# Sample attention scores and value products in plain float32 matmuls, without splits

## The chip, the cores and the metric

The kernel runs on one core of a Trainium2 chip. The metric is the device time of one execution in microseconds; the median of three runs stands for a kernel. Engines are named as in the profile: PE (matrix multiply), PEld (its weight loads), DVE (vector), ACT (scalar), POOL (GpSimd), SP (the queue that issues the transfers).

## The reference

One inference step of a one-layer hybrid encoder: 1024 prompt frames of one new stream and 16 new frames for each of 8 running streams, model width 1024. The change touches the attention of the running streams (the sample): 8 heads of 64, 512 cached frames per stream plus the 16 new ones, no softmax but a stick-breaking weight:

```python
z = jnp.einsum('bqhd,bkhd->bhqk', q, k) * (HEAD_DIM ** -0.5)
log_fail = jnp.where(mask, jax.nn.log_sigmoid(-z), 0.0)
log_between = lax.cumsum(log_fail, axis=3, reverse=True) - log_fail
a = jnp.where(mask, jnp.exp(jax.nn.log_sigmoid(z) + log_between), 0.0)
return jnp.einsum('bhqk,bkhd->bqhd', a, v)
```

Everything is float32. Around it lie an input projection, the same attention over the prompt, a pooling branch, gates, an output projection, and a convolutional feed-forward part.

## The kernel before

All tokens (128 sample rows and 1024 prompt rows) go through the input projection, the pooling branch, the prompt attention, then the sample attention woven with branch A of the later tokens, the output projection and the feed-forward part, one after the other on one core.

**Precision by splits.** PE multiplies operands of type `F32R` in one pass. To keep float32 precision the kernel splits a tensor into a high part, a copy into an `F32R` tile, and a low part, the difference (`split`, L85), and replaces a product by three matmuls: high × high, high × low, low × high (`mm3`, L118; L119 to L121 in the profile). An operand that is not `F32R`, such as the data of a transpose against the identity, is multiplied in plain float32.

**The sample attention** works on one stream (a batch b, 0 to 7) at a time, with keys in pairs of heads (p, 0 to 3):

- `s_kload` and `s_vload` issue the loads of cached keys (1 MB) and values (4 × 256 KB) on SP.
- `s_kt` (L781) transposes a pair's 512 keys on PE into a PSUM bank; `s_kth` (L794, ACT) copies it as the high part `kth`, `s_ktl` (L799, DVE) subtracts for the low part `ktl`. Only then the bank is free. `s_new` (L788, DVE) appends the 16 new keys to both.
- `s_qb` (L775, POOL) lays a batch's queries, high and low, into a block-diagonal tile `qb`.
- `s_qk` forms the scores `zs` with `mm3`: columns 256 to 527 first (n = 1, 272 columns), then 0 to 255 (n = 0), four pairs each, 12 matmuls a half. The chain `chain_steps` (L600 to L612) follows: three ACT functions, a sum, a scan and a sum on DVE, an exponential on ACT.
- `s_tr` (L822) transposes the weights on PE; `s_a3` copies their high part (L833, ACT) and subtracts the low part (L831, DVE).
- `s_vh` (L761, DVE) casts a value tile to its high part, `s_vl` (L765, mostly POOL) makes the low part, in tiles borrowed from `mh12`, `ml12` and the prompt's buffers.
- `s_av` multiplies for each quarter j of the keys and each pair: one matmul of both weight parts (64 columns of weights) with the high values (L847), one of the high weights (32 columns) with the low values (L851). `s_ob` and `s_os` bring the four parts out, `s_sum` adds them.

Between these stand `br_half`, the halves of branch A (six split matmuls of 384 columns each), whose results go through `merge_unit`: a gate product (L938, DVE), a sum (L939, POOL), a copy (L940, ACT) and a low part (L941, DVE).

**The order** of this stage is written by hand. Each step is put into a list with a due time (`at_(time, function)`), the list is sorted, and every engine runs its own steps in that order (`tc.manual_schedule`). A period of one batch is 10.6 in these times; they set the order only. Batches 0 to 2 overlap without branch work before batch 2; from batch 2 on a period holds a batch's scores, four key transposes of the next, four branch halves, four value products of the one before, and one transpose of weights.

Of the kernel before, what the change touches and what calls it, by code (L numbers as in the profile page):

```python
# [16 lines left out]
P = 128  # L17
# [22 lines left out]
def trunk_kernel(  # L40
# [421 lines left out]
    s_samp = ExitStack()  # L462
    smp = mk_pool("samp", "left", stack=s_samp)
    qs_h = smp.tile([P, 4, P], F32R, name="qs_h")
    qs_l = smp.tile([P, 4, P], F32R, name="qs_l")
    ks_h = smp.tile([P, 4, P], F32R, name="ks_h")
    ks_l = smp.tile([P, 4, P], F32R, name="ks_l")
# [8 lines left out]
    def qkv_units(p):  # L476
# [66 lines left out]
        def k_tr(ts_):  # L543
# [180 lines left out]
    def s_setup():  # L724
        for i in range(2):
            q_ = p2.tile([P, 2, AW], F32R, tag="ql", bufs=2, name=f"qb{i}")
            for j in range(2):
                pool.memset(f32(q_[:, j, :]), 0.0)
            qb.append(q_)
# [15 lines left out]
    def s_vload(b, j):  # L745
        if b == 6 and j < 2:
            if j == 0:
                vt["x"] = p2.tile([P, 4, AW], F32R, tag="vhl", bufs=2, name="v6")
            vt[b, j] = vt["x"][:, j, :], vt["x"][:, 2 + j, :]
        elif b % 2 == 0:  # L750
            vt[b, j] = mh12[:, 4 + j, :AW], ml12[:, 4 + j, :AW]
        else:
            if j == 0 and b == 1:
                vt["qd"] = [p2.tile([P, 2, AW], F32R, tag=f"qd{k}", bufs=2, name=f"v{'lh'[k]}{b}_{i}")
                            for k in range(2) for i in range(2)]
            vt[b, j] = vt["qd"][j // 2][:, j % 2, :], vt["qd"][2 + j // 2][:, j % 2, :]
        vr[b, j] = p2.tile([P, AW], F32, tag="kvst", bufs=4, name=f"vr{b}_{j}")
        sync.dma_start(vr[b, j], cache_v[0, b, j * P:(j + 1) * P].rearrange("p h d -> p (h d)"))

    def s_vh(b, j):  # L760
        dve.tensor_copy(vt[b, j][1], vr[b, j])  # L761

    def s_vl(b, j):
        lo, hi = vt[b, j]
        (dve if (b == NB - 1 and j > 1) or (b in (4, 6) and j == 0) else pool).tensor_tensor(lo, vr.pop((b, j)), f32(hi), ALU.subtract)  # L765

    def s_qb(b):
        for j, src in enumerate((qs_h, qs_l)):
            for hh in range(2):
                hs = slice(hh * HD, (hh + 1) * HD)  # L770
                q_ = qb[b % 2]
                sv = f32(src[hs].rearrange("p a (t b) -> p a t b", b=NB)[:, :, :, b])
                c0, o = (384, P) if j else (0, 0)
                dst = q_.rearrange("p j c -> p (j c)")[hs, c0:c0 + 640].rearrange("p (a s) -> p a s", s=160)
                pool.tensor_copy(dst[:, :, o + hh * NS:o + (hh + 1) * NS], sv)  # L775
# [8 lines left out]
    def s_new(b, i):  # L784
        for j, (hl, src) in enumerate((("h", ks_h), ("l", ks_l))):
            kt = p2.tile([P, 2, KA], F32R, tag=f"kk{j}", bufs=2, name=f"kt{hl}{b}_{i}")
            bst[b].setdefault(hl, []).append(kt)
            dve.tensor_copy(kt[:, :, PAST:KA],  # L788
# [715 lines left out]
```

## Time and profile before

| | us |
|---|---|
| median of 3 runs | 1776.23 (1775.72 to 1777.47) |
| span of the profiled execution | 1774.7 |
| PE busy in it | 1708.0 |
| sample attention, first cached-key transpose to output projection | 652.10 to 797.76 |

The page gives the profiled execution's span, from its first to its last instruction; a time of its own beside the span is not shown, and the span lies 1.5 us under the median. Times are microseconds from the start of the span. A busy time counts instructions that run; matmuls overlap, so PE may be busy without being at its peak, and the distance of two starts, not the duration, says what a matmul costs in a row of them. "PEclk" is the share of full clock that PE was granted: 1.00 is 2.4 GHz, 0.50 is 1.2 GHz, and a value between is a mean over a stretch with both. What stands behind an arrow is the instruction that ended a wait.

### The profile page before, as it was taken

To read this page: it belongs to the slowest core of one execution; us is meant where nothing else is said; L and a number is where in the kernel's file an instruction comes from. 1 tells how busy PE (TensorE), PEld (TensorE's weight loads), DVE (VectorE), ACT (ScalarE), POOL (GpSimd) and SP (SyncE) were. 2 spreads that over 40 slices of the span, in tenths; PEclk is the share of its full clock that TensorE was granted. 3 is DMA by queue.
4 is the path that set the end of the run, shared out by engine and by line. 5 is a ranking of instruction groups with operands and counts; after the bars stand their busy time and mean duration, and the time that the engine had idled before them with its cause. 6 is when DMAs were issued, how large, how long until landed. Compare 5 with 4: busy or idle time off the path is not lost.

```text
span 1774.7 us, 24393 instructions
## 1 busy us (share of the span) xinstructions
PE 1708.0 (96%) x9785; PEld 1565.1 (88%) x9785; DVE 936.5 (53%) x1311; ACT 753.4 (42%) x1472; POOL 487.9 (27%) x506
## 2 busy tenths in 40 slices
PE   8999999999999997779999999999999999999997
PEld 7999998888888886778889998989989898998995
DVE  5350117778776778894253535345353444535356
ACT  5231127777776775543234332423223242332423
POOL 5111233222222125552412222322213131222222
PEclk9999999999999998989999999999999999999999
DMA  6111131111113125548301110211111111110112
GB/s 184 49 49 63 63 102 54 51 47 39 50 53 119 61 88 201 161 148 267 101 13 36 37 48 24 60 36 48 39 36 48 48 37 47 36 51 25 60 36 110
DMA packets 132942, 125.39 MB, mean 71 GB/s; under 512 B 8625, under 2 KB 113021, under 8 KB 132829
## 3 DMA queue, kind: packets, MB, share of 16 engines
q1 hardware_dynamic: 132829, 123.83, 22.4%
q8 instruction: 77, 1.26, 0.3%
q14 instruction: 36, 0.29, 0.1%
HBM read 101.63 MB, written 21.65 MB: 69 GB/s over the span
## 4 chain that ended last, share of the span: by engine, by line
PE 75%; DVE 15%; ACT 4%; DMA 2%; issue 2%; POOL 1%; SPq 0%; POOLq 0%; DVEq 0%; ACTq 0%
PE up L121 10%; PE up L119 10%; PE up L120 10%; PE dn L119 4%; PE dn L120 4%; PE dn L121 4%; DVE S L607 2%; PE gb L120 2%; PE gb L121 2%; PE gb L119 2%; PE kv L119 2%; PE kv L121 1%; PE kv L120 1%; PE o L119 1%; PE o L120 1%
## 5 line engine op out<-in xcount | busy, mean ns | idle before, releaser
L119 PE MATMUL up<-mh,wup_h 128*128 128x384 f32 x1056 | 353.4, 335 | 0.0
L121 PE MATMUL up<-mh,wup_l 128*128 128x384 f32 x1056 | 353.0, 334 | 0.0
L120 PE MATMUL up<-ml,wup_h 128*128 128x384 f32 x1056 | 352.8, 334 | 0.0
L1371 DVE SCALAR_TENSOR_TENSOR C<-E,convp,C 128x128 f32<-128x128 f32 x88 | 80.4, 913 | 287.1 <-ACT C L1368 278.5
L1428 DVE TENSOR_TENSOR x<-dn,x 128x512 f32<-128x512 f32 x198 | 132.8, 687 | 149.8 <-PE dn L121 149.7
L119 PEld LDWEIGHTS up<-mh,wup_h 128*128 128x128 f32 x1056 | 198.4, 188 | 0.5
L120 PEld LDWEIGHTS up<-ml,wup_h 128*128 128x128 f32 x1056 | 198.3, 188 | 0.3
L121 PEld LDWEIGHTS up<-mh,wup_l 128*128 128x128 f32 x1056 | 198.3, 188 | 0.0
L96 POOL TENSOR_TENSOR wup_l<-wup_r,wup_h 128x1024 fp32r<-128x1024 f32 x44 | 104.9, 2393 | 283.9 <-ACT wup_h L95 244.5
L119 PE MATMUL dn<-wd_h,gh 128*128 128x512 f32 x396 | 158.4, 401 | 2.0 <-DVE x L1428 2.0
L120 PE MATMUL dn<-wd_l,gh 128*128 128x512 f32 x396 | 156.5, 395 | 1.4 <-POOL wd_l L96 1.4
L121 PE MATMUL dn<-wd_h,gl 128*128 128x512 f32 x396 | 156.3, 395 | 0.0
L95 ACT CAST wup_h<-wup_r 128x1024 fp32r<-128x1024 f32 x44 | 45.5, 1050 | 212.8 <-PE dn L121 143.5
L1367 ACT COPY E<-up 128x384 f32<-128x384 f32 (+2 forms) x176 | 65.6, 398 | 151.0 <-PE up L121 151.0
L1372 DVE SCALAR_TENSOR_TENSOR C<-E,convp,C 128x1024 f32<-128x1024 f32 x88 | 112.0, 1273 | 0.0
L119 PEld LDWEIGHTS dn<-wd_h,gh 128*128 128x128 f32 x396 | 74.2, 188 | 25.9 <-DVE x L1428 9.2
L120 PEld LDWEIGHTS dn<-wd_l,gh 128*128 128x128 f32 x396 | 74.4, 188 | 18.5 <-POOL wd_l L96 1.9
L121 PEld LDWEIGHTS dn<-wd_h,gl 128*128 128x128 f32 x396 | 74.4, 188 | 17.9
L1368 ACT ACTIVATE C<-up,convp 128x384 f32<-128x384 f32 x132 | 90.0, 682 | 0.0
L605 DVE SCALAR_TENSOR_TENSOR e<-z,e 128x384 f32<-128x384 f32 (+3 forms) x96 | 53.2, 554 | 62.1 <-ACT e L602 61.4
L119 PE MATMUL kv<-wkv_h,hTh 128*128 128x256 f32 x288 | 85.0, 295 | 0.9 <-DVE ql L506 0.9
L96 POOL TENSOR_TENSOR wd_l<-wd_r,wd_h 128x1024 fp32r<-128x1024 f32 x22 | 52.9, 2403 | 105.0 <-ACT wd_h L95 105.0
(324 smaller groups left out, 4099.7 us busy)
## 6 DMA issues: line engine op xcount, KB each, us to landing
wup_r<-in_w_up_dram SPq DMA_DIRECT2D x44, 512.0 KB
wd_r<-in_w_down_dram SPq DMA_DIRECT2D x22, 512.0 KB
vr<-in_cache_v_dram SPq DMA_DIRECT2D x32, 256.0 KB
kr<-in_cache_k_dram SPq DMA_DIRECT2D x7, 1024.0 KB
sp_tb<-tb SPq DMA_DIRECT2D x8, 576.0 KB
out_dram<-kvst SPq DMA_DIRECT2D x72, 64.0 KB
sp_ga<-ga SPq DMA_DIRECT2D x24, 192.0 KB
tbr<-sp_tb SPq DMA_DIRECT2D x24, 192.0 KB
```

The source lines that it names most:

```text
L95: act.copy(hi, raw)
L96: (pool if how[1] == "p" else dve).tensor_tensor(lo, raw, f32(hi), ALU.subtract)
L119: pe.matmul(ps, lhsT=lh, rhs=rh, start=start, stop=False)
L120: pe.matmul(ps, lhsT=lh, rhs=rl, start=False, stop=False)
L121: pe.matmul(ps, lhsT=ll, rhs=rh, start=False, stop=stop)
L605: dve.scalar_tensor_tensor(ev, z, 0.0, ev, ALU.max, ALU.add)
L607: dve.tensor_tensor_scan(Sv[:, ::-1], ev[:, ::-1], ev[:, ::-1], init, ALU.add, ALU.bypass)
L1367: act.copy(d_, s2_)
L1368: act.activation(C[:, cs], ps, AF.Identity, scale=convp[:, 2, u:u + 1], bias=convp[:, 3, u:u + 1])
L1371: dve.scalar_tensor_tensor(C[:, 0:P], E[:, 16 - 8 * sh:EZ - 8 * sh], wv, C[:, 0:P], ALU.mult, ALU.add)
L1372: dve.scalar_tensor_tensor(C[:, P:T], E[:, EP - sh:EL - sh], wv, C[:, P:T], ALU.mult, ALU.add)
L1428: ins = dve.tensor_tensor(x1[t][:, hs], ps, x1[t][:, hs], ALU.add)
```

## The change

Queries, keys, values and weights of the sample stay plain float32, in one tile each. `mm3` in `s_qk` becomes one plain matmul for each pair, the two value matmuls become one with 32 columns of weights, and all low parts and casts of the sample go. A transposed key block is copied once, by ACT for even and by DVE for odd pairs; the weights' first half by ACT, the second by DVE. Values are loaded straight into the tiles that the matmul reads (two sets, so a load waits for the value products of two batches before). A batch's queries are laid out by eight small POOL copies. The due times of the steps that stay are unchanged.

```diff
-                act.activation(qs_h[:, p, :], ps[:, 0:P], AF.Copy, scale=SCALE)
-                dve.scalar_tensor_tensor(qs_l[:, p, :], ps[:, 0:P], SCALE, f32(qs_h[:, p, :]),
-                                         ALU.mult, ALU.subtract)
+                act.activation(qs[:, p, :], ps[:, 0:P], AF.Copy, scale=SCALE)
...
-                split(ks_h[:, p, :], ks_l[:, p, :], tp)
+                act.copy(ks[:, p, :], tp)
...
-        vr[b, j] = p2.tile([P, AW], F32, tag="kvst", bufs=4, name=f"vr{b}_{j}")
+        vr[b, j] = vb(b, j)
         sync.dma_start(vr[b, j], cache_v[0, b, j * P:(j + 1) * P].rearrange("p h d -> p (h d)"))
 
-    def s_vh(b, j):
-        dve.tensor_copy(vt[b, j][1], vr[b, j])
-
-    def s_vl(b, j):
-        lo, hi = vt[b, j]
-        (dve if (b == NB - 1 and j > 1) or (b in (4, 6) and j == 0) else pool).tensor_tensor(lo, vr.pop((b, j)), f32(hi), ALU.subtract)
+    def vb(b, j):
+        if j % 2 == 0:
+            vt[b, j // 2] = p2.tile([P, 2, AW], F32, tag=f"qd{j // 2}", bufs=2, name=f"v{b}_{j}")
+        return vt[b, j // 2][:, j % 2, :]
...
+            for a in range(4):
+                o = a * 160 + hh * NS
+                pool.tensor_copy(qb[b % 2][hs, o:o + NS], sv[:, a, :])
...
-        act.copy(d_["h"][i][:, p % 2, :PAST], d_["tp", p])
-
-    def s_ktl(b, p):
-        d_ = bst[b]
-        i = p // 2
-        dve.tensor_tensor(d_["l"][i][:, p % 2, :PAST], d_.pop(("tp", p)), f32(d_["h"][i][:, p % 2, :PAST]), ALU.subtract)
+        (act.copy if p % 2 == 0 else dve.tensor_copy)(d_["k"][p // 2][:, p % 2, :PAST], d_.pop(("tp", p)))
...
-            mm3(z[:, :w], qb[b % 2][:, 0, pc], qb[b % 2][:, 1, pc],
-                d_["h"][p // 2][:, p % 2, kc], d_["l"][p // 2][:, p % 2, kc], p == 0, n == 0 and p == 3)
+            pe.matmul(z[:, :w], lhsT=qb[b % 2][:, pc], rhs=d_["k"][p // 2][:, p % 2, kc],
+                      start=p == 0, stop=n == 0 and p == 3)
...
-        if lo:
-            dve.tensor_tensor(a3[:, :, :, 1, :], src, f32(a3[:, :, :, 0, :]), ALU.subtract)
-        else:
-            act.copy(a3[:, :, :, 0, :], src)
+        (dve.tensor_copy if i else act.copy)(d_["a3"][i], src)
...
+            pe.matmul(av[:, p, :], lhsT=d_["a3"][j // 2][:, j % 2, p, :], rhs=v[:, p * P:(p + 1) * P],
+                      start=(j == 0 and p == 0), stop=(j == 3 and p == 3))
...
-    def s_sum():
-        dve.tensor_tensor(osum[0], osum[0], osum[1], ALU.add)
```

What this does to the order is seen on DVE at the beginning of batch 5's period. Before, between the gate product of the period that ends and the first key block of batch 6 (`gar` is a gate, `vr` the loaded values of batch 4, `ml` and `mh` the tiles lent to their high and low part, `ks` the new keys):

```order
L1056 CAST wa_0_hi<-wa_0_raw 128x1024
L938 TENSOR_TENSOR gar_7028<-br_a_2_7729,gar_7028 128x384
L761 CAST ml_6854<-vr_0_7613 128x512
L765 TENSOR_TENSOR mh_6853<-vr_0_7613,ml_6854 128x512
L761 CAST ml_6854<-vr_1_7617 128x512
L761 CAST ml_6854<-vr_2_7641 128x512
L761 CAST ml_6854<-vr_3_7644 128x512
L788 CAST kth_0_7844<-ks_h 128x2x16
L788 CAST ktl_0_7846<-ks_l 128x2x16
L788 CAST kth_1_7848<-ks_h 128x2x16
L788 CAST ktl_1_7850<-ks_l 128x2x16
L799 TENSOR_TENSOR ktl_0_7846<-tr_kc_0_7852,kth_0_7844 128x512
```

The same place after the change, where `kt` is the one tile of keys:

```order
L1011 CAST wa_0_hi<-wa_0_raw 128x1024
L894 TENSOR_TENSOR gar_6981<-br_a_2_7498,gar_6981 128x384
L767 COPY kt_0_7573<-ks 128x2x16
L767 COPY kt_1_7575<-ks 128x2x16
L897 TENSOR_TENSOR ml_6842<-gar_6981,mh_6841 128x384 x2
L772 COPY kt_0_7573<-tr_kc_1_7601 128x512
L601 SCALAR_TENSOR_TENSOR es_1_7547<-zs_1_7541,es_1_7547 128x272
```

Five operations on values and two on keys are gone from between the gate product and the batch's sum and scan, and the key block of pair 1 has come in as a copy.

On PE, at the end of batch 3's period and the scores of batch 4, before (`avs` value products of batch 2, `tr_as` weights of batch 3, `zs_1` the 272-column half):

```order
L847 MATMUL avs_7468<-ml_6854,a_2_1_7351 64x128
L822 MATMUL tr_as_7573<-ident,es_0_7431 128x128 x2
L822 MATMUL tr_as_7573<-ident,es_1_7401 128x128 x2
L119 MATMUL zs_1_7582<-kth_0_7442,qb_5855 128x272
L120 MATMUL zs_1_7582<-ktl_0_7444,qb_5855 128x272
L121 MATMUL zs_1_7582<-kth_0_7442,qb_5855 128x272
```

and after:

```order
L813 MATMUL avs_7292<-v_2_7144,a_2_1_7215 32x128 x4
L795 MATMUL tr_as_7380<-ident,es_0_7264 128x128 x2
L795 MATMUL tr_as_7380<-ident,es_1_7250 128x128 x2
L783 MATMUL zs_1_7389<-kt_0_7271,qb_5845 128x272 x2
L783 MATMUL zs_1_7389<-kt_1_7273,qb_5845 128x272 x2
L787 LDWEIGHTS rep_121
```

Eight value matmuls of a quarter have become four, twelve score matmuls of a half four; their places among the transposes and branch halves are the same.

## Rows read from the trace of the kernel before

**Rows 1.** The page, part 1: busy us, share of the span, instructions.
```profile
PE 1708.0 (96%) x9785; PEld 1565.1 (88%) x9785; DVE 936.5 (53%) x1311; ACT 753.4 (42%) x1472; POOL 487.9 (27%) x506
```

**Rows 2.** Windows: length; us (records) of PE, PEld, DVE, ACT, POOL; PEclk, DMA share, GB/s.
```profile
652.10:672.39 20.29, 15.77 (x112) 13.17 (x111) 16.95 (x34) 11.89 (x27) 11.38 (x11) 1.00 0.77 280
672.39:694.94 22.55, 18.97 (x141) 17.80 (x139) 18.91 (x33) 13.03 (x33) 11.76 (x10) 0.77 0.50 163
694.94:714.46 19.52, 13.32 (x105) 12.49 (x103) 15.34 (x24) 11.81 (x22) 9.91 (x11) 0.91 0.47 150
714.46:732.79 18.33, 14.28 (x104) 13.44 (x103) 15.28 (x27) 7.61 (x20) 12.30 (x12) 0.81 0.62 193
732.79:748.83 16.04, 11.94 (x104) 11.29 (x103) 15.53 (x25) 10.98 (x21) 7.84 (x9) 1.00 0.64 197
748.83:766.88 18.05, 14.14 (x104) 13.55 (x103) 14.24 (x26) 7.60 (x20) 11.98 (x12) 0.81 0.53 164
766.88:797.76 30.88, 24.60 (x177) 22.73 (x176) 29.42 (x41) 16.95 (x30) 15.58 (x13) 0.94 0.39 108
797.76:812.00 14.24, 14.24 (x66) 11.77 (x65) 7.00 (x10) 3.57 (x5) 0.68 (x1) 1.00 1.04 351
```

**Rows 3.** What PE waited for, 652.10 to 797.76: us in total, times, longest us.
```profile
PE tr_kc L781 <- DVE ktl L799: 10.7, 3, 4.0
PE br_a L119 <- DVE gar L938: 7.6, 2, 5.4
PE avs L847 <- DVE a L831: 7.0, 2, 3.5
PE tr_as L822 <- DVE ktl L799: 5.1, 3, 3.0
PE tr_as L822 <- ACT es L612: 0.2, 1, 0.2
```

**Rows 4.** DVE in the stage, then groups by shape: count, busy us, mean ns, idle before.
```profile
652.10:797.76 145.66, 125.68 (x206) 0.89 0.55 173
...
L799 DVE TENSOR_TENSOR ktl<-tr_kc,kth 128x512 fp32r<-128x512 f32 x32 | 21.3, 683 | 7.9 <-ACT kth L794 7.8
L761 DVE CAST vh<-vr 128x512 fp32r<-128x512 f32 x16 | 15.0, 980 | 0.0
L761 DVE CAST ml<-vr 128x512 fp32r<-128x512 f32 x14 | 12.2, 920 | 0.0
L788 DVE CAST kth<-ks_h 128x32 fp32r<-128x32 f32 x14 | 8.8, 629 | 2.4 <-PE zs L121 2.4
L607 DVE TENSOR_TENSOR_SCAN Ss<-es 128x272 f32<-128x272 f32 x8 | 8.7, 1089 | 0.3
L831 DVE TENSOR_TENSOR a<-tr_as,a 128x256 fp32r<-128x256 f32 x16 | 6.0, 414 | 6.0 <-ACT a L833 6.0
```

**Rows 5.** Single PE instructions: start, us, line, tile, count; then two lines' min/median/max ns.
```profile
660.05 0.28 PE L121 MATMUL zs<-kth,qb 128*128 128x256 f32 x1
...
661.24 1.91 PE L781 MATMUL tr_kc<-ident,kr 128*128 128x128 f32 x16
...
775.09 0.23 PE L851 MATMUL avs<-mh,a 128*32 128x128 f32 x1
...
775.57 0.39 PE L119 MATMUL br_a<-ah,wa_hi 128*128 128x384 f32 x1
...
796.22 1.89 PE L889 MATMUL avt<-a3t,vs 128*128 128x256 f32 x8
...
L889 PE MATMUL avt<-a3t,vs x8: 378/379/379, 796.2 to 797.7; 128*128 128x256 f32 x8
L781 PEld LDWEIGHTS tr_kc<-ident,kr x128: 138/140/231, 651.9 to 766.2; 128*128 128x128 f32 x128
```

**Rows 6.** PE in order of time at the kernel's start.
```profile
7.58 1.97 PE L148 MATMUL tr_a<-ident,xn 128*128 128x128 f32 x8 [1.61 <-DVE xn L249]
...
11.85 2.08 PE L267 MATMUL u<-hTh,wu_h 128*128 128x256 f32 x8
```

More of the change, by code (lines that the diff above doesn't have):

```diff
@@ L725, in s_setup @@
         for i in range(2):
-            q_ = p2.tile([P, 2, AW], F32R, tag="ql", bufs=2, name=f"qb{i}")
-            for j in range(2):
-                pool.memset(f32(q_[:, j, :]), 0.0)
+            q_ = p2.tile([P, AW], F32, tag="ql", bufs=2, name=f"qb{i}")
+            pool.memset(q_, 0.0)
             qb.append(q_)
@@ L823, in s_tr, with s_a3 @@
         d_["ta"] = tp
-        d_["a3"] = [p2.tile([P, 2, 4, 2, 2 * NS], F32R, tag="ah", bufs=3, name=f"a3_{b}_{i}") for i in range(2)]
-    def s_a3(b, i, lo):
+        d_["a3"] = [p2.tile([P, 2, 4, 2 * NS], F32, tag="ah", bufs=3, name=f"a3_{b}_{i}") for i in range(2)]
+    def s_a3(b, i):
         d_ = bst[b]
         src = d_["ta"][:, 2 * i:2 * i + 2, :].rearrange("p n (a r) -> p n a r", a=4)
-        a3 = d_["a3"][i]
-        if lo:
-            dve.tensor_tensor(a3[:, :, :, 1, :], src, f32(a3[:, :, :, 0, :]), ALU.subtract)
-        else:
-            act.copy(a3[:, :, :, 0, :], src)
+        (dve.tensor_copy if i else act.copy)(d_["a3"][i], src)
     def s_av(b, j):
@@ L837, in s_av @@
         if j == 0:
-            d_["av"] = psp.tile([4 * NS, 4, P], F32, tag="av", bufs=1, name=f"avs{b}")
+            d_["av"] = psp.tile([2 * NS, 4, P], F32, tag="av", bufs=1, name=f"avs{b}")
             if b == 0:
-                osum.extend(p2.tile([P, 4, 2, HD], F32, tag="e", bufs=6, name=f"os{i}") for i in range(2))
+                osum.append(p2.tile([P, 4, 2, HD], F32, tag="e", bufs=6, name="os"))
         av = d_["av"]
-        i, n = j // 2, j % 2
-        vl, vh = vt.pop((b, j))
-        a3 = d_["a3"][i]
+        v = vr.pop((b, j))
         for p in range(4):
-            pc = slice(p * P, (p + 1) * P)
-            both = lambda: pe.matmul(av[:, p, :], lhsT=a3[:, n, p].rearrange("p a r -> p (a r)"), rhs=vh[:, pc],
-                                     start=(j == 0 and p == 0), stop=(j == 3 and p == 3))
-            if j == 0:
-                both()
-            pe.matmul(av[0:2 * NS, p, :], lhsT=a3[:, n, p, 0, :], rhs=vl[:, pc], start=False, stop=False)
-            if j:
-                both()
+            pe.matmul(av[:, p, :], lhsT=d_["a3"][j // 2][:, j % 2, p, :], rhs=v[:, p * P:(p + 1) * P],
+                      start=(j == 0 and p == 0), stop=(j == 3 and p == 3))
     def s_ob(b):
         d_ = bst.pop(b)
-        ob = p2.tile([4 * NS, 4, P], F32, tag="e", bufs=6, name=f"ob{b}")
+        ob = p2.tile([2 * NS, 4, P], F32, tag="e", bufs=6, name=f"ob{b}")
         act.copy(ob, d_["av"])
@@ L861, in s_os @@
     def s_os(b):
-        for pl in range(2):
-            for hh in range(2):
-                r0 = (2 * pl + hh) * NS
-                dst = osum[pl].rearrange("(t b) a h d -> b t a h d", b=NB)[b, :, :, hh, :]
-                sync.dma_start(dst, obs[b][r0:r0 + NS, :, hh * HD:(hh + 1) * HD])
+        for hh in range(2):
+            dst = osum[0].rearrange("(t b) a h d -> b t a h d", b=NB)[b, :, :, hh, :]
+            sync.dma_start(dst, obs[b][hh * NS:(hh + 1) * NS, :, hh * HD:(hh + 1) * HD])
     tail = {}
@@ L1110, in trunk_kernel @@
                 th = (3.0, 4.7, 7.0, 8.9) if late else (3.9, 5.3, 7.0, 9.65)
-                tl = (3.5, 4.72, 7.5, 9.4) if late else (4.5, 6.1, 7.5, 10.0)
                 at_(o + th[p], s_kth, b + 1, p)
-                at_(o + tl[p], s_ktl, b + 1, p)
         if b < NB:
@@ L1131, in trunk_kernel @@
             if b < NB:
-                tn = 0.2 if b == 0 else 14.0 if b == 1 else o + (8.6 if b == NB - 1 else PER)
                 tv = -1.0 + 0.01 * p if b == 0 else (5.1 if b == 1 else 16.15 if b == 2 else o + 1.05) + 0.3 * p
-                th, tl = tn + 0.7 + 0.3 * p, tn + (1.0 if b != 1 else 2.1) + 0.3 * p
                 at_(tv, s_vload, b, p)
-                if p == 0 and late and b < NB - 1:
-                    th, tl = o + 9.3, o + 9.35
-                if b in (4, 6) and p == 0:
-                    tl = th + 0.05
-                at_(th, s_vh, b, p)
-                at_(tl, s_vl, b, p)
         if b > 0:
```

43 lines of the change are left out of this document (10 added, 33 removed).

## The prediction, made before the changed kernel was run

> **What bounds the kernel now.** I read the page first: PE is busy for 96% of the span, DVE for 53% [rows 1]. A mean over stages settles nothing, so I cut the sample attention into windows, from the first transpose of cached keys (652.10 us) over the score matmuls of batches 2 to 7 to the first matmul of the output projection (797.76 us) [rows 2]. Look at the PE and DVE columns beside each window's length. PE's busy times of the seven windows add up to 113.0 us of 145.7: it stands idle for 32.6 us, while DVE is busy for 125.7 [rows 4]; the fifth window, 16.04 us long, holds 15.53 us of DVE work. From 797.76 us on PE is busy without a gap, so whatever the stage gains or loses reaches the end of the kernel.
>
> Then the list of what PE waited for [rows 3]. Nearly all of it is DVE: the low half of a transposed key block (L799), which holds the PSUM buffer that the next transposes want; the low half of the weights (L831); and the gate multiply L938, itself a short operation, that stands in DVE's queue behind the casts of cached values. The exponential at the end of the softmax chain ended 0.2 us of waiting. The stage is bound by DVE's queue, and PE pays for it twice: behind its longer waits the granted clock falls to the lower of its two levels, 1.2 GHz, seen as a mean of 0.77 to 0.94 in five windows [rows 2].
>
> **What goes.** From DVE [rows 4]: 32 low halves of keys (21.3 us), the casts of cached values (15.0 + 12.2, and a few smaller groups), the new keys' copies (8.8), the low halves of the weights (6.0): 63.3 us in the groups shown. What comes to DVE is bounded from above by the same rows: 16 key copies that ACT did before, at 0.683 = 10.9; 16 copies of new keys at the longer form's 0.629 = 10.1; 8 weight copies at 0.414 = 3.3. DVE is left with at most 125.7 − 63.3 + 24.3 = 86.7 us. ACT loses 16 key copies and 8 weight copies of its 79.9 us in the seven windows; POOL loses the subtractions of the values and gets small copies of queries (8 instead of 4 per batch), placed a period before the scores that need them. None of these comes near the length of the stage.
>
> **What comes to PE.** A plain float32 matmul appears in the trace before in one place with 128 weight columns, L889: four instructions of 256 columns left eight records, over 1.89 us with a last one of 0.379, so a record is (1.89 − 0.379)/7 = 0.216 us and a matmul two of them, 0.432 [rows 5]. The split matmul of 256 columns comes every (661.24 − 660.05)/10 = 0.119 us, three of them 0.357. Scores: 4 × (0.432 − 0.357) = 0.30 us for the 256-column half of a batch, 0.32 for the 272 columns by the same ratio, 0.62 × 8 batches = 5.0 us more. Value products: the split pair takes 2 × (775.57 − 775.09)/8 = 0.120 us. For a 128-column plain pass the nearest row is the float32 transpose, (1.91 − 0.272)/15 = 0.109 us, half of 0.216; two passes are 0.218. So 16 × (0.218 − 0.120) = 1.57 us a batch, 12.5 us in all. Bounds: the new weights have 32 columns, so a pass can hardly cost less than its 0.108 of columns; if the weight load of 0.140 us [rows 5] were not hidden, 256 passes would cost 7.9 us more. I take 0.109, since under the same load the transposes come every 0.109. Sum: **PE gets 17.5 us more work**, 17.5 to 25.4.
>
> Here a page of the Trainium skill prices the same thing otherwise: "FP8 and Floating Point Precision", section "TensorE Precision Notes", says true FP32 takes four passes through the array. Four times the split matmul's interval would be 0.476 us for 256 columns against the measured 0.432, and by it the extra would be 7.9 for scores and 15.4 for values, 23.3 us, the forecast 5.8 us later. The row decides; the sum goes by it.
>
> **What PE has left at full clock.** Windows 4, 5 and 6 hold the same 104 matmul records; the one at clock 1.00 takes 11.94 us, the other two 14.28 and 14.14 and the third 13.32 [rows 2]. The lower clock costs 2.34 + 2.20 + 1.38 = 5.9 us there. In window 2 the mean of 0.77 means 2 × 0.23 × 22.55 = 10.4 us at the lower level, half of which is lost: 5.2; in the last, likewise, 1.9. Together 13.0 us. So PE's work is 113.0 − 13.0 = 100.0 us at 2.4 GHz, and 117.5 with the new passes. Against the 145.7 us of the stage the floor of the change is **a gain of 28.2 us**, if no wait and no low clock is left.
>
> **What is late next.** PE itself. In a period after the change PE has 11.94 + 0.62 + 1.57 = 14.1 us of work; DVE, by the cut above, at most 86.7/8, ACT less. The order keeps PE's distances: between a batch's scores and the transposes of its weights lie three or four key transposes, branch halves and value products, 7 to 9 us of PE work, against a chain of four short ACT steps, two scans of up to 1.089 and four sums; with 0.5 for each step, about that of the weights' operation (0.414), that is some 6 us, an estimate from [rows 4]. The new wait: the key copies of odd pairs now stand on DVE, with the scans queued behind them, and PE's next transposes or scores wait for them. In the first three batches no branch work covers that: I allow one copy (0.68) at each of the three scores, 2 us, and in four later periods and the tail about 0.8 us each, 4 us. Loads of values now wait for the value products of two batches before (the buffer), not for POOL's subtraction; behind them on SP stand the key load and gate loads, due a period later. The first window moves data for 0.77 × 20.29 = 15.6 us of full transfer time [rows 2], so it can't shrink under that; I have it at about 18. Two result transfers per batch and the last sum go; PE had work beside them.
>
> So 28.2 − 6 = 22.2 us of gain. The rows are of an execution with a span of 1774.7 us; the median of the runs is 1776.2, 1.5 us around the span, which I leave as it is: 1776.2 − 22.2 = **1754.0 us**.
>
> **The rivals.**
> 1. *The waits come back in another place.* Every queue is in program order, and the order was kept from a program in which DVE was late everywhere. If half of the 32.6 us stays as waits on copies, scans or gates, the gain is 28.2 − 16.3 = 11.9, less up to 3 us of clock: 1764 to 1767. For it: DVE and ACT copies now both sit in one PSUM ring. Against: DVE's load falls by a third, and ACT ended only 0.2 us.
> 2. *Plain passes don't hold the clock*, the case on the slow side. At the kernel's start eight transposes took 1.97 us, where sixteen take 1.91 later, and the eight split matmuls of 256 columns behind them 2.08 us, where eight take about 1.0 later [rows 5, 6]: they ran at the lower level, and it had not risen over the transposes. After the change the first three batches hold hardly anything but plain passes and transposes: three scores at 3.57, a value product of 3.5, three sets of key transposes, some 20 us. If those run at 1.2 GHz they take 20 us more and the gain is gone (1774). From 22 us of such work at the lower level the change is a loss; all 74 us of it (28.6 scores, 28 values, 17.5 transposes) would give 1754 + 74 = 1828. Against: the first window, with transposes, scores and waits under 3 us, keeps a clock of 1.00, and from the third batch on 192 split branch matmuls stand between the plain ones.
> 3. *The waits are not the splits'.* If the idle time is the batch chain's own and stays, PE's passes simply add: 1776.2 + 17.5 = 1793.7. Against: the releasers in rows 3 are removed instructions or stand behind them.
> 4. *The plain matmuls don't cost what L889 shows*, with 32 weight columns a pass being shorter, or DVE's relief also frees the prompt's end: below 1748.
>
> **Chances.** Forecast, 1748 to 1760: 0.60. Rival 1: 0.24. Rival 2: 0.08, of it 0.05 slower and 0.02 even. Rival 3: 0.04. Rival 4: 0.04. The likeliest is the forecast. The range goes from the floor's 1748 up to rival 1's 1767, leaving out about 0.16. A measurement of this kernel can tell about 0.2% (3.6 us) from no change: faster 0.88, same 0.03, slower 0.09.
>
> **What would show it.** Right: in the stage PE's idle time under 8 us, granted clock 1.00, DVE busy under 87 us, records of 0.216 at the scores and pairs of 0.218 at the value products, about 118 to 124 us from the first cached-key transpose to the output projection, and the same times behind it. Wrong: a wait of several us on a copy or scan in each period (rival 1), a granted clock of 0.5 over stretches in which PE was busy (rival 2), idle time as long as before (rival 3), or a value pass longer than 0.14 us.

## The result, and the profile after

The changed kernel takes **1757.39 us** (median of 4 runs, 1755.44 to 1760.64) against 1776.16 for the kernel before on the same chip: a ratio of 0.989, 95% interval 0.9876 to 0.9904, or 18.8 us less. The forecast was 1754.0, the range 1748 to 1767. The profiled execution has a span of 1755.9 us (1774.7 before).

The sample attention, from the first cached-key transpose to the first matmul of the output projection, now lies from 653.84 to 777.21 us: 123.4 us instead of 145.7. This is the page's first part after the change, which answers to [rows 1] (busy us, share of the span, instructions):

```profile
PE 1718.8 (98%) x9721; PEld 1563.8 (89%) x9721; DVE 884.6 (50%) x1226; ACT 744.3 (42%) x1448; POOL 447.7 (25%) x508
```

And the windows by stage, cut at the scores of each batch as in [rows 2] (length; us and records of PE, PEld, DVE, ACT, POOL; PEclk, DMA share, GB/s):

```profile
653.84:671.72 17.88, 15.51 (x96) 12.58 (x95) 12.21 (x20) 9.54 (x22) 5.76 (x11) 1.00 0.77 279
...
690.68:705.60 14.92, 14.92 (x95) 12.26 (x95) 8.54 (x17) 11.05 (x20) 7.06 (x13) 1.00 0.59 180
705.60:720.35 14.75, 14.75 (x95) 12.13 (x93) 7.43 (x17) 6.02 (x15) 3.26 (x10) 1.00 0.73 250
...
750.02:777.21 27.19, 27.19 (x167) 23.90 (x167) 16.57 (x27) 16.46 (x28) 8.39 (x8) 1.00 0.44 136
```

Compare the first two numbers of each row. From the second window on, PE is busy for the whole window, at a granted clock of 1.00; before, PE was idle for 32.6 us and five of seven windows had a mean clock under 1. A period, 16.0 to 19.5 us before, now takes 14.92 or 14.75. What PE waited for in the stage, where [rows 3] had 30.6 us (us in total, times, longest):

```profile
PE tr_as L795 <- ACT es L608: 2.2, 1, 2.2
PE av L672 <- DVE al L87: 0.2, 1, 0.2
```

DVE, at 125.7 us before, is busy for 73.2. Its groups now (count, busy us, mean ns, idle before), beside [rows 4]:

```profile
L772 DVE COPY kt<-tr_kc 128x512 f32<-128x512 f32 x16 | 10.8, 687 | 11.4 <-PE tr_kc L761 11.4
L897 DVE TENSOR_TENSOR ml<-gar,mh 128x384 fp32r<-128x384 f32 x15 | 10.1, 687 | 10.0 <-ACT mh L896 10.0
...
L767 DVE COPY kt<-ks 128x32 f32<-128x32 f32 x12 | 6.0, 539 | 0.0
```

DVE now waits for PE before the key copies (11.4 us): the roles have changed. What PE does in a quarter of a period (start, us, line, tile, count):

```profile
705.60 2.00 PE L783 MATMUL zs<-kt,qb 128*128 128x272 f32 x8
...
707.63 1.99 PE L783 MATMUL zs<-kt,qb 128*128 128x256 f32 x8
709.47 0.60 PE L761 MATMUL tr_kc<-ident,kr 128*128 128x128 f32 x4
709.82 0.42 PE L119 MATMUL br_a<-ah,wa_hi 128*128 128x384 f32 x1
...
711.04 1.06 PE L813 MATMUL avs<-v,a 128*32 128x128 f32 x8
712.04 0.66 PE L761 MATMUL tr_kc<-ident,kr 128*128 128x128 f32 x4
```

The distances of the starts are the prices. A batch's scores take 709.47 − 705.60 = 3.87 us. Eight value records take 712.04 − 711.04 = 1.00; inside the block they come every (1.06 − 0.273)/7 = 0.112 us (0.273 is the median duration of one). A split branch half takes 711.04 − 709.82 = 1.22 us. The same place in the one full period before that ran at clock 1.00 (the fifth window of [rows 2]):

```profile
736.44 0.42 PE L119 MATMUL br_a<-ah,wa_hi 128*128 128x384 f32 x1
...
737.56 0.22 PE L847 MATMUL avs<-ml,a 128*64 128x128 f32 x1
...
738.04 0.60 PE L781 MATMUL tr_kc<-ident,kr 128*128 128x128 f32 x4
```

There the branch half took 1.12 us and the eight split value records 0.48.

### The profile page after: what moved, and what is told of

Same layout as the page of the kernel before. It is cut to its first block, busy times and chain, and to the rows that moved or that the text cites. A ratio compares the mean times of both kernels' runs of the same rounds, so it can differ in the third digit from the quotient of the medians.

```text
span 1755.9 us, 24096 instructions
## 1 busy us (share of the span) xinstructions
PE 1718.8 (98%) x9721; PEld 1563.8 (89%) x9721; DVE 884.6 (50%) x1226; ACT 744.3 (42%) x1448; POOL 447.7 (25%) x508
## 4 chain that ended last, share of the span: by engine, by line
PE 78%; DVE 12%; ACT 4%; DMA 2%; issue 2%; POOL 1%; SPq 0%; POOLq 0%; ACTq 0%; DVEq 0%
PE up L121 10%; PE up L120 10%; PE up L119 10%; PE dn L119 4%; PE dn L120 4%; PE dn L121 4%; DVE S L603 3%; PE gb L120 2%; PE gb L121 2%; PE gb L119 2%; PE avs L813 2%; PE zs L783 2%; PE ga L119 2%; PE ga L121 1%; PE o L119 1%
## 5 line engine op out<-in xcount | busy, mean ns | idle before, releaser
L121 PE MATMUL kv<-wkv_h,hTl 128*128 128x256 f32 x288 | 81.4, 283 | 0.0
```

What stands on the lines that cost most here:

```text
L121: pe.matmul(ps, lhsT=ll, rhs=rh, start=False, stop=stop)
```

## Experiments

The table holds the stage of each profiled execution (first cached-key transpose to output projection), PE's and DVE's busy time in it, the mean granted clock, and the median time with its ratio to the kernel before on the same chip.

| | stage | PE busy | PE idle | DVE busy | POOL busy | clock | time, us | ratio (95%) |
|---|---|---|---|---|---|---|---|---|
| before | 145.7 | 113.0 | 32.6 | 125.7 | 80.7 | 0.89 | 1776.2 | |
| the change | 123.4 | 121.0 | 2.4 | 73.2 | 39.1 | 1.00 | 1757.4 | 0.989 (0.9876 to 0.9904) |
| the change again | 121.3 | 121.0 | 0.3 | 69.3 | 39.6 | 1.00 | 1757.2 | 0.9893 (0.9875 to 0.9912) |
| DVE copies put back | 126.1 | 122.8 | 3.3 | 100.0 | 42.0 | 0.99 | 1759.4 | 0.9899 (0.9885 to 0.9914) |
| the same and POOL's work | 141.6 | 126.9 | 14.7 | 124.7 | 85.6 | 0.95 | 1777.6 | 0.9998 (0.9988 to 1.0007) |
| DVE copies threefold | 164.4 | 134.0 | 30.4 | 154.0 | 42.4 | 0.91 | 1798.3 | 1.012 (1.0103 to 1.0137) |
| scores plain only | 131.7 | 110.4 | 21.3 | 113.9 | 83.5 | 0.95 | 1763.1 | 0.992 (0.9905 to 0.9934) |
| values plain only | 123.1 | 118.1 | 5.0 | 83.7 | 39.4 | 1.00 | 1755.6 | 0.9882 (0.9867 to 0.9896) |
| value splits on ACT and DVE | 124.9 | 110.5 | 14.4 | 93.6 | 46.1 | 0.95 | 1759.3 | 0.9895 (0.9881 to 0.991) |
| one value block | 121.1 | 117.1 | 4.0 | 72.2 | 39.1 | 1.00 | 1753.3 | 0.9859 (0.9844 to 0.9873) |
| eight value blocks | 128.9 | 127.7 | 1.2 | 70.3 | 39.4 | 1.00 | 1764.4 | 0.9923 (0.9908 to 0.9937) |
| scores in one pass | 110.0 | 103.7 | 6.3 | 70.8 | 40.9 | 0.97 | 1744.6 | 0.9818 (0.9802 to 0.9835) |
| one block, later transposes | 121.2 | 117.4 | 3.8 | 70.0 | 39.1 | 1.00 | 1755.3 | 0.9878 (0.9861 to 0.9894) |
| values plain, one block | 125.9 | 118.0 | 7.9 | 81.4 | 38.7 | 0.97 | 1758.0 | 0.989 (0.9875 to 0.9905) |

### Was DVE's queue the bound?

**DVE copies put back.** To the whole change, 64 copies are added to DVE's queue at the due times of the casts of values and of the low halves of keys.

```diff
+    def s_junk():
+        dve.tensor_copy(jk, qs.rearrange("p a c -> p (a c)"))
...
                 at_(o + th[p], s_kth, b + 1, p)
+                at_(o + ((3.5, 4.72, 7.5, 9.4) if late else (4.5, 6.1, 7.5, 10.0))[p], s_junk)
...
+                tn = 0.2 if b == 0 else 14.0 if b == 1 else o + (8.6 if b == NB - 1 else PER)
+                at_(tn + 0.7 + 0.3 * p, s_junk)
```

> The whole change, with 64 copies of 128 x 512 from one fixed tile into another put into DVE's queue where the casts of values and the low halves of keys stood; nothing reads their result, and no other engine waits for them. At 0.95 us each, as the casts of values took, they are 61 us: DVE 80 + 61 = 141 us of work in a stage that lasts 123. If DVE's queue was the bound of the kernel before, the stage becomes as long as DVE's work or longer, 141 to 150 us, and the time 1775 to 1785: the gain is gone with PE's work and all transfers unchanged. If the gain came from shorter chains between engines or buffers that come free sooner, the time stays within 5 us of 1757.

It measured 1759.41 us, within 5 us of the change, so by what was written the theory of DVE's queue had lost. But the load wasn't the one meant. DVE's group of the added copies (count, busy us, mean ns):

```profile
L772 DVE CAST jk<-qs 128x512 fp32r<-128x512 f32 x58 | 33.4, 575 | 0.9
```

The window of the whole stage, columns as above:

```profile
652.38:778.44 126.06, 122.81 (x763) 102.12 (x762) 100.04 (x190) 70.73 (x145) 42.04 (x74) 0.99 0.61 202
```

A cast of the same shape and types took 0.980 and 0.920 us in the kernel before [rows 4]; here the mean is 0.575 and the median of all 60 in the trace 0.427. DVE came to 100 us instead of 141, in a stage of 126. One place in the trace showed what may make them longer. DVE in order of time (start, us):

```profile
665.68 2.50 DVE L768 COPY kt<-ks 128x32 f32<-128x32 f32 x2
```

And POOL at the same time:

```profile
664.56 2.35 POOL L958 TENSOR_TENSOR al<-ml,ah 128x768 fp32r<-128x768 f32 x1 [3.20 <-ACT ah L955]
```

Two copies of 32 elements a partition, 0.27 us for the pair in another place of this trace, took 2.50 while POOL had a subtraction running.

The trace of the kernel before holds the same pair of prices, which the reading of [rows 4] as a price passed over. Two casts of values on DVE:

```profile
768.90 1.28 DVE L761 CAST v<-vr 128x512 fp32r<-128x512 f32 x1
...
771.52 0.41 DVE L761 CAST v<-vr 128x512 fp32r<-128x512 f32 x1
```

And POOL at the same time:

```profile
768.59 1.30 POOL L1059 TENSOR_TENSOR wa_lo<-wa_raw,wa_hi 128x512 fp32r<-128x512 f32 x1 [4.62 <-DVE wa_hi L1056]
769.85 1.20 POOL L939 TENSOR_TENSOR gar<-gar,tbr 128x384 f32<-128x384 f32 x1
772.07 1.35 POOL L765 TENSOR_TENSOR v<-vr,v 128x512 fp32r<-128x512 f32 x1 [1.02 <-issue]
```

The first cast ran beside the first two POOL operations, the second between the second and the third. Of the 32 casts in that stage, the four that no POOL instruction overlaps took 0.41 us each; the others have a median of 1.24. The low halves of keys, which read one operand from PSUM, took 0.68 with and without POOL beside them; so where an added copy stands for one of those, about 0.26 us of the missing load is the copy's own and not POOL's.

**DVE copies and POOL's subtractions.** So the next kernel adds to this one 32 subtractions on POOL, at the due times of the low halves of values, on tiles that nobody else writes.

```diff
+    def s_junkp():
+        pool.tensor_tensor(jp, qs.rearrange("p a c -> p (a c)"), ks.rearrange("p a c -> p (a c)"), ALU.subtract)
...
+                at_(tn + (1.0 if b != 1 else 2.1) + 0.3 * p, s_junkp)
```

> The extra DVE copies of the run before this one took 0.42 us each and not 0.95, so DVE had only 100 us of work in 126 and the stage did not lengthen. Here the same 64 copies stand with 32 subtractions of 128 x 512 on POOL at the places where POOL made the low halves of the values; nothing reads the results of either. If the casts of values were long in the kernel before because POOL worked beside them (in that run a pair of small DVE copies took 2.50 us while POOL had a 2.35 us operation running): the copies near the subtractions take 0.9 us and more, DVE's busy time rises by 12 to 25 us over 100, and the stage lengthens to 128 to 140 us, time 1760 to 1773. If POOL does not touch DVE: copies stay at 0.42, DVE at about 100, time 1757 to 1760.

1777.55 us, and a stage of 141.6: both a little above what was written (1760 to 1773, 128 to 140). The whole gain is gone, ratio 0.9998. It isn't the old state in each part: PE is idle for 14.7 us, not 32.6, and the plain matmuls' extra work makes up for most of the difference. Against the run before, PE has no instruction more, and none waits for what was added. DVE's instructions are those of the run before, but its busy time is 24.7 us longer. The stage's window:

```profile
653.90:795.49 141.59, 126.90 (x764) 105.73 (x762) 124.74 (x190) 69.79 (x144) 85.64 (x105) 0.95 0.54 179
```

Its DVE groups:

```profile
L773 DVE CAST jk<-qs 128x512 fp32r<-128x512 f32 x59 | 49.5, 838 | 0.9
L905 DVE TENSOR_TENSOR ml<-gar,mh 128x384 fp32r<-128x384 f32 x14 | 14.2, 1033 | 0.3 <-ACT mh L904 0.3
L780 DVE COPY kt<-tr_kc 128x512 f32<-128x512 f32 x16 | 10.9, 684 | 8.9 <-PE tr_kc L763 8.9
```

The added copies went from 0.575 to 0.838 us and the low part of the gated branch (L905) to 1.033 from 0.692; the key copies, which read PSUM, stayed at 0.684. DVE in order of time:

```profile
739.45 1.39 DVE L773 CAST jk<-qs 128x512 fp32r<-128x512 f32 x1
740.76 1.37 DVE L769 COPY kt<-ks 128x32 f32<-128x32 f32 x2
742.05 0.42 DVE L773 CAST jk<-qs 128x512 fp32r<-128x512 f32 x1
...
745.02 0.41 DVE L773 CAST jk<-qs 128x512 fp32r<-128x512 f32 x1
```

And POOL in the same stretch:

```profile
739.21 4.40 POOL L776 TENSOR_TENSOR jp<-qs,ks 128x512 fp32r<-128x512 f32 x3
743.55 2.26 POOL L757 COPY qb<-qs 64x16 f32<-64x16 f32 x8
```

The three subtractions take 1.47 us each. The copy that started beside the first of them took 1.39 us; the one at 742.05, where the second ends (740.68 + 1.47 = 742.15), 0.42, and the one at 745.02, with no subtraction running, 0.41.

**DVE copies threefold**, with nothing on POOL, so that DVE's own work exceeds PE's:

```diff
-        dve.tensor_copy(jk, qs.rearrange("p a c -> p (a c)"))
+        for _ in range(3):
+            dve.tensor_copy(jk, qs.rearrange("p a c -> p (a c)"))
```

> The whole change with 192 copies of 128 x 512 on DVE, three at each of the 64 places of the earlier run, and nothing more on POOL. At 0.42 us each they are 81 us: DVE 73 + 81 = 154 us of work, more than PE's 121. If DVE's queue as such can bound the stage: it lasts 150 to 165 us, time 1783 to 1800. If what bound the kernel before was POOL's and DVE's mutual hindrance and not the length of DVE's queue: time under 1765.

1798.28 us, at the upper end of what was written, and the stage follows DVE, as its window shows:

```profile
652.22:816.60 164.38, 133.97 (x764) 109.55 (x762) 153.96 (x309) 69.72 (x144) 42.42 (x73) 0.91 0.47 154
```

The three runs together: DVE's queue bounds the stage when its work comes near PE's (125 us against 127) or exceeds it, and at 100 us of 126 it doesn't. In the kernel before it came there by its own operations and by POOL's subtractions, which stretched them.

### Which half of the change brings the gain?

**Scores plain only.** From the kernel before, `s_qk`, `s_new`, `s_kth` and `s_qb` become those of the change and `s_ktl` goes; the values keep their split.

```diff
-            mm3(z[:, :w], qb[b % 2][:, 0, pc], qb[b % 2][:, 1, pc],
-                d_["h"][p // 2][:, p % 2, kc], d_["l"][p // 2][:, p % 2, kc], p == 0, n == 0 and p == 3)
+            pe.matmul(z[:, :w], lhsT=qb[b % 2][:, pc], rhs=d_["k"][p // 2][:, p % 2, kc],
+                      start=p == 0, stop=n == 0 and p == 3)
```

> Only the scores are plain float32; the value products keep their split, with the casts of cached values on DVE. If DVE's queue bounded the kernel before: DVE in the stage falls from 125.7 us by the 32 low halves of keys (21.3) and the low copies of new keys, and rises by 16 key copies (10.9), to about 105; PE's work is 100.0 + 5 = 105 us. The two are level, so about half of the old waits should stay: stage 115 to 128 us, time 1753 to 1765. If the casts of values alone were the trouble: nearly all 32.6 us of idle time stay and the time is about 1776 + 5 = 1781. If DVE is out of the way altogether: 1742 to 1748, faster than both kernels.

1763.05 us, as the first theory had it, though the stage of 131.7 us lies above its 115 to 128. DVE still has 113.9 us of work, where about 105 were expected, and PE waits for it (us in total, times, longest):

```profile
PE avs L833 <- DVE a L817: 8.0, 2, 4.5
PE tr_as L808 <- DVE kt L785: 5.5, 2, 3.1
PE br_a L119 <- DVE gar L924: 4.0, 2, 2.8
```

**Values plain only.** The other half: `s_vload`, `s_a3`, `s_av`, `s_ob` and `s_os` of the change; `s_vh`, `s_vl` and `s_sum` go; keys and queries keep their split.

```diff
-                pe.matmul(av[0:2 * NS, p, :], lhsT=a3[:, n, p, 0, :], rhs=vl[:, pc], start=False, stop=False)
...
+                pe.matmul(av[:, p, :], lhsT=d_["a3"][j // 2][:, j % 2, p, :], rhs=v[:, p * P:(p + 1) * P],
+                          start=(j == 0 and p == 0), stop=(j == 3 and p == 3))
```

> Only the value products are plain float32; the scores keep their split with the low halves of keys on DVE. DVE in the stage: 125.7 less the casts of values (27.2) and the low halves of weights (6.0), plus 8 weight copies (3.3), about 94 us; PE's work 100.0 + 18 (the blocks of eight value records took 0.99 us in the changed kernel against 0.48) = 118 us. If PE is the bound as soon as DVE has room: stage 120 to 127, time 1753 to 1760, about that of the whole change. If the low halves of keys (15.8 us of the waits that ended on them) are what matters: at least 10 us of waits stay and the time is 1764 to 1772.

1755.61 us. This half alone brings all of the gain (its interval overlaps that of the whole change, so which of the two is shorter isn't settled). PE's waits in its stage:

```profile
PE tr_as L809 <- DVE ktl L786: 3.0, 1, 3.0
PE zs L120 <- DVE ktl L786: 1.1, 2, 0.8
```

Before, the low halves of keys (L799) ended 16.7 us of waiting, the 15.8 of [rows 3] and 0.9 at the scores. All 32 are still there, and end 4.1. Those 32 take 0.68 us each as before, so they were late because of what stood ahead of them, the casts of values, stretched by POOL's subtractions, and not by their own length.

**Value splits on ACT and DVE.** Scores plain, values split, but POOL has none of the subtractions:

```diff
     def s_vh(b, j):
-        dve.tensor_copy(vt[b, j][1], vr[b, j])
+        act.copy(vt[b, j][1], vr[b, j])
...
-        (dve if (b == NB - 1 and j > 1) or (b in (4, 6) and j == 0) else pool).tensor_tensor(lo, vr.pop((b, j)), f32(hi), ALU.subtract)
+        dve.tensor_tensor(lo, vr.pop((b, j)), f32(hi), ALU.subtract)
```

> Scores in plain float32, value products split as before, but the high parts of the values are made by ACT (32 copies at about 0.58 = 19 us) and the low parts by DVE (32 at about 0.68 = 22 us), and POOL has none of them. Estimates from the traces: PE 100.0 + 5 = 105 us, DVE 73 + 22 + 7 for the low halves of the weights = 102, ACT 70 + 19 = 89, POOL 39. If each engine's own load decides and POOL no longer stretches DVE's copies, PE bounds the stage at 105 plus up to 10 us of waits: stage 107 to 116, time 1741 to 1751, faster than the whole change with the same precision. If the waits of the first run (scores plain alone, 21 us idle) come from the order of the steps and not from load: stage 122 to 130, time 1757 to 1764.

1759.33 us, by the second theory. No engine is full (PE 110.5, DVE 93.6, ACT 88.3 us of 124.9), and still PE stands idle for 14.4 us. Its waits:

```profile
PE br_a L119 <- DVE gar L924: 5.1, 1, 5.1
PE avs L833 <- DVE a L817: 4.3, 2, 2.2
```

The longest wait is one of 5.1 us behind a gate product in DVE's order, which points to the order, and not the sum of a queue, as what this version would have to mend. No run shows that.

### What do the plain matmuls cost PE?

**One block of value products in a period** instead of four, in batches 1 to 6:

```diff
-                at_(tb_ + 1.4, s_av, b - 1, p)
+                at_(o + 2.8 + 1.85 * 3 + 1.4 + 0.01 * p, s_av, b - 1, p)
```

> The whole change, with the four value products of a period in one run of 32 records instead of four of 8, in batches 1 to 6; nothing else moves. In the changed kernel eight records take 0.99 us up to the next instruction where 8 x 0.112 = 0.90, and a branch half ahead of them 1.22 us where 1.13 was. If this 0.2 us belongs to the entry into and the exit from a block of plain matmuls, three blocks less in six periods save 18 x 0.2 = 3.6 us: stage about 120 us, time 1753 to 1755. If it belongs to each plain record, nothing changes: 1757.

1753.33 us. PE's busy time falls from 121.00 to 117.13: 3.87 us for 18 blocks fewer, 0.215 each, as the first theory said. PE here, in order of time:

```profile
698.28 3.11 PE L813 MATMUL avs<-v,a 128*32 128x128 f32 x27
...
706.04 0.42 PE L119 MATMUL br_a<-ah,wa_hi 128*128 128x384 f32 x1
...
707.17 0.60 PE L761 MATMUL tr_kc<-ident,kr 128*128 128x128 f32 x4
```

In the long block, of whose 32 records the last 27 are in this view, a record comes every (3.11 − 0.273)/26 = 0.109 us, and a branch half with transposes on both sides takes 707.17 − 706.04 = 1.13.

**Eight blocks**, the opposite: each quarter cut in two, half ahead of the branch half and half behind it.

```diff
-                at_(tb_ + 1.4, s_av, b - 1, p)
+                at_(tb_ + 0.45, s_av, b - 1, p, (0, 1))
+                at_(tb_ + 1.4, s_av, b - 1, p, (2, 3))
```

> The whole change, with each quarter's value product cut in two, four records before the branch half and four behind it, in batches 1 to 6. If 0.2 us belongs to the entry and exit of each block of plain value matmuls: 4 more blocks in six periods cost 24 x 0.2 = 4.8 us, less if the first half joins the key transposes ahead of it without a cost; time 1758 to 1762. If it belongs to each record: no change, 1757.

1764.35 us, more than the 1758 to 1762 written for it: PE's busy time rises by 6.70 us for 24 blocks more, 0.28 each. PE has the same passes in all three versions; only the number of edges differs (places where one kind of matmul follows another), and PE's work goes with it, 117.1, 121.0, 127.7 us.

**Scores in one pass.** Keys and queries are rounded to `F32R` and no low part is kept, so the scores have that precision only:

```diff
-            q_ = p2.tile([P, AW], F32, tag="ql", bufs=2, name=f"qb{i}")
+            q_ = p2.tile([P, AW], F32R, tag="ql", bufs=2, name=f"qb{i}")
...
-        kt = p2.tile([P, 2, KA], F32, tag=f"kk{i}", bufs=2, name=f"kt{b}_{i}")
+        kt = p2.tile([P, 2, KA], F32R, tag=f"kk{i}", bufs=2, name=f"kt{b}_{i}")
```

> The whole change, but the score matmuls take keys and queries rounded to F32R, one pass and no low part (the scores are then only as precise as F32R operands; that part of the computation is changed). DVE, ACT and POOL do the same copies. A batch's scores take 3.87 us on PE in the changed kernel and would take 8 x 0.12 = 1.0. If PE is the bound after the change, the stage shortens by about 2.8 x 8 = 22 us less a few us of new waits: time 1735 to 1742. If copies, scans or exponentials set the pace and PE only fills their time, the gain is under 5 us: 1752 to 1757.

1744.60 us: between the two figures, and far from the second theory. PE is the bound after the change, but not for all of the 22 us that were offered. In the steady part a batch's scores take 1.37 us (702.49 to 703.86) for 3.87, as PE in order of time shows:

```profile
702.49 0.75 PE L783 MATMUL zs<-kt,qb 128*128 128x272 f32 x4
...
703.27 0.75 PE L783 MATMUL zs<-kt,qb 128*128 128x256 f32 x4
703.86 0.60 PE L761 MATMUL tr_kc<-ident,kr 128*128 128x128 f32 x4
```

That is 2.5 × 8 = 20 us. The first two windows of its stage gave part of it back:

```profile
653.88:670.00 16.12, 11.28 (x81) 9.43 (x79) 9.36 (x20) 9.57 (x23) 5.43 (x11) 0.92 0.75 265
670.00:686.00 16.00, 16.00 (x106) 13.46 (x105) 10.11 (x18) 10.12 (x25) 6.22 (x11) 0.87 0.89 315
```

PE is idle for 4.8 us in the first (3.9 of them in one wait for the exponential of batch 0), and the mean clock of these two windows is lower, 0.92 and 0.87. In the whole stage 5.1 us of PE's work ran at the lower level, so about half of that, 2.6 us, is lost. 20 − 2.6, less 4.0 us of more idle time in the stage, is 13.4, and the stage is 13.4 us shorter.

### Two attempts at a shorter version

**One block, later transposes**: the kernel with one value block, and the first batch's weight transposes placed behind the scores of batch 2.

```diff
-            tt = 9.75 if b == 0 else 16.15 if b == 1 else o + (PER + 0.55 if b == NB - 1 else 9.8 if late else 8.45)
+            tt = 12.95 if b == 0 else 16.15 if b == 1 else o + (PER + 0.55 if b == NB - 1 else 9.8 if late else 8.45)
```

> The whole change with one block of value products per period (1753.3 when alone), and the first batch's weight transposes moved behind the scores of batch 2, since PE waited 2.3 us for an exponential there. If the chain of batch 0 is late only for that place: the wait goes, stage 119 us, time about 1751. If the wait only moves to the scores of batch 2 or to the value products of batch 0: 1753.

1755.26 us, no gain over one block alone: the wait moved, as the second theory had it. Its stage has as much idle time (3.8 us), in other places, as PE's waits show:

```profile
PE tr_kc L761 <- DVE a L802: 1.1, 1, 1.1
PE tr_as L795 <- DVE kt L772: 0.9, 3, 0.4
```

**Values plain, one block**: both due times above in the kernel with plain values only.

> Scores split as before, value products plain in one block per period, and the first weight transposes moved as in the run above. PE: 118 us of the run with plain values alone less 3.6 for the blocks = 114.5; its 4.7 us of waits less the one of 3.0 at the first weight transposes if it goes. If PE still bounds the stage: 115 to 119 us, time 1746 to 1751, faster than every version with full precision so far. If the low halves of keys on DVE become late now that the value block comes at the end of the period: over 8 us of waits, 1753 or more.

1757.99 us, by the second theory, with 7.9 us of idle time: PE should have been busy for less than the 118.1 us of the version without the block, but waited more and ran at a mean clock of 0.97, and was busy for 118.0. Its waits:

```profile
PE zs L120 <- DVE ktl L786: 3.5, 2, 2.8
PE tr_as L809 <- DVE ktl L786: 1.7, 3, 0.6
```

**The change again**, unaltered, for the time ahead of the stage.

> The changed kernel once more, unaltered. Its first profile reached the sample attention 1.74 us later than the kernel before, with the same PE instructions ahead of it, and the eleven runs since reached it anywhere between 649.99 and 657.49 us. If that is a difference between executions: the stage is again 123.4 us long within 0.5, and begins at another time in that range. If the change itself delays the prompt part: it begins at 653.8 again, within 0.3. Time 1754 to 1760 either way.

It reached the stage at 654.59 us, and the stage took 121.3 us, 2.1 less than in the first profile: the one wait for an exponential, 2.2 us there, is 0.2 here. So neither sentence was quite right: the start is one of many in the range, and the stage itself varies by 2 us through that wait. PE's busy time is 121.00 in both.

The shortest version without a product in one rounded pass is the one with one value block: 1753.33 us, at a ratio of 0.9859 against 0.989 and 0.9893. Its interval ends where that of the change begins (0.9873 and 0.9876; 0.9875 in the repeat), and the same block with later transposes gave 0.9878, so the gain is likely but at the limit of what these runs tell.

## Why the prediction was right, and which terms were off

**The bound: right as to the engine, incomplete as to the reason.** DVE's queue held PE up, and with DVE's load gone the waits went. But the prediction took the 0.98 and 0.92 us of the casts as their price, and wrote of POOL only that it lost its subtractions. The trace of before and the runs with added work show that the same copies cost 0.41 to 0.42 us without POOL, and that as many of them bring the old time back only with POOL's subtractions beside them. The Trainium skill has this in "SBUF — State Buffer", section "SBUF: two separate sides": POOL and DVE share a pair of SBUF ports, and of a POOL operation and a DVE operation that needs the pair (one in a two-port mode, or, against a POOL operation that reads SBUF, one with two inputs there) the one that starts first holds it to its end while the other blocks. The traces agree: a copy from SBUF takes 0.42 against 1.39 us beside a subtraction, the low part of the gated branch with its two SBUF inputs goes from 0.692 to 1.033, and a copy from PSUM isn't touched (0.684 to 0.687 us in the change and in all three runs with added copies).

**DVE after: right as a bound.** At most 86.7 us were forecast; 73.2 and 69.3 were measured. The difference lies mostly in two places. Smaller groups of the splits also went and had not been subtracted (9.7 us in the trace of before: the low copies of new keys, 2.9, and casts and low parts of values in other tiles). And the copies of new keys, 16 at 0.629 us in the bound, are 12 in the stage, at 0.539 in the first profile and 0.249 in the repeat, which is also nearly all that separates the two profiles.

**PE's extra work: the step that was mis-sized.** 17.5 us were forecast, with 25.4 as the upper end; PE went from 100.0 to 121.0, so 21.0. The 100.0 was an estimate, and it holds: of PE's busy time before, 26.2 us fall into stretches of granted clock 0.5, and 113.0 less half of them is 99.9. The single halves price the two terms. Scores: PE's 110.4 us at a mean clock of 0.95 hold 0.05 × 131.7 = 6.6 us of low clock, so 103.8 at full clock, 3.8 us more, where 5.0 was forecast (the change less values plain only, both at clock 1.00, gives 121.0 − 118.1 = 2.9). Values: 118.1 at clock 1.00, **18.1 us more where 12.5 was forecast**, the term that failed in size. A period, put at 14.1 us of PE work, holds 14.75 to 14.92. The record's price was right, 0.109 us inside a long block and 0.112 in one of eight. What the sum left out are the edges: eight records in a block of eight take 1.00 us and not 0.87, and a branch half ahead of them 1.22 and not 1.12 or 1.13. Before, a block of eight split value records took 0.48 us, just its records. The pair of versions with one and eight blocks shows it, at 0.215 and 0.28 us a block. The upper end had been worked out from another cause, an unhidden weight load, which the 0.109 in the long block shows not to be there.

By the page "FP8 and Floating Point Precision" of the Trainium skill, section "TensorE Precision Notes", with its four passes, the extra would have come to 23.3 us. The measured 21.0 lies between that and the forecast. But the four passes would lie in each record, and the measured surplus lies at the blocks' edges.

**The waits: also off, to the other side.** 6 us were allowed; 2.4 and 0.3 us were measured. The allowed 0.68 at each early score, and 0.8 in each period, didn't come. So the stage, forecast at 145.7 − 22.2 = 123.5 us, took 123.4 and 121.3. That the first fits to 0.1 us is luck: PE's work was 3.5 us too small and the waits 3.6 too large, and in the repeat 5.7 too large. The first window, put at about 18 us, took 17.88.

**The clock: right.** It stayed at 1.00 in every window, over the first 18 us of transposes and plain scores too, and rival 2 is gone. Of the kernel's start, on which that rival rests, the profile prints a granted clock of 1.00 as well (7 to 14 us), but it has no clock record before 14.2 us; that PE ran at the lower level there is worked out from the doubled times alone. The versions in the table whose mean clock fell are those in which PE had waited: the lowest, 0.89 and 0.91, with 32.6 and 30.4 us of idle time.

**"The same times behind it": wrong by 1.7 us.** The output projection comes 20.55 us earlier than before, the end 18.8. What PE waited for from 777 us to 860 us, where before only gate products had made it wait (1.2 us):

```profile
PE br_a L119 <- DVE gar L894: 1.3, 3, 0.5
PE br_a L119 <- ACT wa_h L95: 1.2, 1, 1.2
```

PE now comes to the branch of the first chunk before ACT has made the high part of its weights. The repeat shows the same 1.2 us. That it comes of arriving earlier isn't shown: with scores in one pass PE arrives 13 us earlier still and has no such wait, and with DVE copies threefold, 39 us later than the change, it has 2.2 us of it. The cause stays open. And the stage began 1.74 us later than before, though PE's instructions ahead of it are the same. Fourteen profiled executions of the kernels shown here began it between 649.99 and 657.49 us, with mean clocks of 0.95 to 1.00 from 300 to 400 us: 1.00 in the two that began first (649.99 and 650.12), 0.95 in the two that began last (656.11 and 657.49). So most of that difference is one between executions. Whether a part below 2 us belongs to the change isn't settled. These 3.5 us are the distance from 22.3 us gained in the stage to 18.8 us in all, and the forecast's 1754.0 missed by them.

**The rivals.** Rival 1 (waits elsewhere) didn't happen, with 2.4 us of idle time. Rival 3 (the splits not the cause) falls with the runs that add DVE's and POOL's work alone: the idle time comes back, 14.7 us with DVE's and POOL's, 30.4 with DVE's threefold. Rival 4 (plain matmuls cheaper with 32 weight columns) falls with 0.109 to 0.112 us per record.

## What to carry to other kernels

A duration in a profile is a price only under the neighbours it had: before a removed operation's time is counted as gain, look at what ran on POOL beside it, and before a releaser is called the cause, look at what stood ahead of it in its queue. Where splits are given up in two products, price each alone: here plain values brought the whole gain, and plain scores beside them none that could be measured. Once PE is the bound, count the edges between kinds of matmul as well as the passes, and put plain products in one run.

## What the runs showed of the hardware that was not expected

- A float32 to `F32R` copy of 128 x 512 from SBUF on DVE takes 0.41 to 0.42 us alone and 1.39 beside a subtraction on POOL; two copies of 32 elements a partition, 0.27 us alone, took 2.50. With 32 subtractions on POOL, 190 recorded DVE instructions of the stage took 124.7 us instead of 100.0.
- A block of plain float32 matmuls between transposes and split matmuls costs 0.21 to 0.28 us beside its passes.
- The stage's length follows DVE's work only near the limit: 27 to 31 us more of DVE work cost 2.7 to 4.8 us of stage (126.1 against 123.4 and 121.3), 81 to 85 us more cost 41 to 43 (164.4).
